# A hybrid attention layer on one core: where GpSimd's sums, the first gate loads and the forget gates' chain stand

## The chip, the cores and the metric

The kernel runs on one core of a Trainium2 chip. The metric is the device time of one execution in microseconds. The engines are named as in the profile: PE is TensorE (PEld its weight loads), DVE is VectorE, ACT is ScalarE, POOL is GpSimd, SP is SyncE, which issues most of the DMAs.

## What is computed

One layer over x of 512 rows by 2048 columns. A combined projection gives the queries, keys, values and z of three attention branches, the logits of the forget gates, and three merge gates of 2048 columns each:

```python
h = jnp.einsum('bsd,dn->bsn', x, w_in) + b_in
p = _split_columns(h)
o_fox = fox_attention(..., p["fox_f"])   # bias: c = cumsum(log_sigmoid(f_logit))
o_swa = swa_attention(...)
o_moba = moba_attention(...)
br_fox = merge(o_fox) * silu(p["fox_z"]) @ w_br_fox      # and so for swa, moba
y = sigmoid(p["gate_fox"]) * br_fox + sigmoid(p["gate_swa"]) * br_swa + sigmoid(p["gate_moba"]) * br_moba
out = y @ w_out
x = layer_norm(ALPHA * x + out)
```

All of it is float32.

## The kernel before

A float32 operand is split into a high part (hi, xh, sh; a copy on ScalarE, rounded to float32r) and a low part (lo, xl, sl; a subtraction on VectorE), and one product is three matmuls: high by high, low by high, high by low. `split` (lines 115 to 117) does that, so nearly every matmul waits for a ScalarE and a VectorE operation on its operands.

The first stages are these. **The first projection** (line 434 on) gives the values of two branches and the forget logits in 32 steps n, 16 for each set of 324 columns: `v_step(n)` runs twelve matmuls, four row blocks by three. `prepare_v(n + 2)` splits the weights two steps ahead and, in the first pass, x tile n + 2; hi and lo have three buffers each. SyncE loads x tiles of 256 KB four steps ahead and weight rows (rawv) six steps ahead. Beside it GpSimd forms sums and differences of pairs of x tiles (`x_sums(g)`, lines 221 to 230, four operations each, eight pairs); `x_sums_split(g)` splits them into sh and sl after the steps in `x_done`, and `s1_split(g)` writes one of them into xh and xl. `v_evac` (line 210) adds the bias rows vb to the result in VectorE, copies four forget logits of each row into the tile fg on GpSimd, and returns the store of the values, which ScalarE's queue issues a step later. The rows vb are loaded by GpSimd's queue.

**The gates** (line 474 on) come in six groups of 56 steps m, seven products of eight steps of six matmuls 128x512. The seven products are those of a Strassen-like scheme over a 2 by 2 block matrix; their operands are the loaded blocks rawa, rawb, rawc and rawd, four of 512 KB each in a group, which VectorE combines in place (`combine`, the table `COMBINE`), and the sums sh. `gate_prepare(n)` splits a block two steps ahead into ghi and glo. After some steps VectorE adds a bank of PSUM and a bias row (gbias) into result tiles, and ScalarE takes the sigmoid and stores them. The tiles of gbias share their two buffers with vb. For the first group SyncE's queue loads a, c and d, GpSimd's queue b; later groups are loaded by SyncE during the group before. rawc takes turns with rawv in four buffers; rawa takes the buffers of the sums' results (xsum), so a load of rawa waits for the split of those.

**The forget gates' chain** `forget_bias` (line 374) computes log sigmoid of the 32 logits in each of 128 rows as a generator in six pieces; a `next` in the last group's steps runs one. Its result goes into the tile pair, and `running_sum` (line 551) forms the cumulative sum by four matmuls on TensorE in the projection behind the gates, whose steps are those of a weight stream (four steps of twelve matmuls for each tile of 128 columns).

The order of all instructions is written by hand: each engine runs its own in the order in which the Python code emits them, and a wait at one of them holds all behind it.

Of the kernel before, what the change touches and what calls it, by code (L numbers as in the profile page):

```python
# [8 lines left out]
F32 = mybir.dt.float32  # L9
F32R = mybir.dt.float32r  # L10
AF = mybir.ActivationFunctionType
ALU = mybir.AluOpType

P = 128
S = 512
# [35 lines left out]
GROUPS = [(b, half) for half in range(2) for b in range(3)]  # L51
# [36 lines left out]
def hybrid_kernel(ctx: ExitStack, tc: tile.TileContext, a: dict, out: bass.AP):  # L88
    nc = tc.nc
# [6 lines left out]
    xl = keep.tile([P, KD, S], F32R, tag="bigl", name="xl")  # L96
    fg = keep.tile([P, 6, 32], F32, name="fg")
# [14 lines left out]
    def att_tile(name):  # L112
        return psum.tile([P, S], F32, tag="att", name=name, bufs=5)
# [11 lines left out]
    def at(i, order, f, *args):  # L125
        tasks.setdefault(i, []).append((order, len(tasks.get(i, ())), f, args))
# [6 lines left out]
    def prepare(i):  # L133

        if i >= len(ids) or i in parts:
            return None
        load(i // 2)
        raw = raws[i // 2][:, (i % 2) * S:(i % 2 + 1) * S]
        if i in held:
            hi, lo = held[i]  # L140
        else:
            hi = stage.tile([P, S], F32R, tag="hi", name="hi")
            lo = stage.tile([P, S], F32R, tag="lo", name="lo")
        parts[i] = (hi, lo)
        nc.scalar.activation(hi, raw, AF.Copy)  # L145

        def lower():
            nc.vector.tensor_sub(lo, raw, hi.bitcast(F32))  # L148
            for d in range(1, raw_bufs):
                load(i // 2 + d)  # L150

        return lower
# [54 lines left out]
    flog = fg[:, 0].rearrange("p (a b) -> p a b", b=NH)  # L207
    vacc = [[acc_tile(f"va{i}") for i in range(3)] + [att_tile("va3")], None]

    def v_evac(ps, st):  # L210
        tag = "qqcp"[st] if ps else "q"
        raw = post.tile([P, S], F32, tag=tag, name="vout", bufs=1 if tag == "c" else 2)[:, :NV]
        nc.vector.tensor_add(raw, vacc[ps][st][:, :NV], vb[ps])
        nc.gpsimd.tensor_copy(flog[:, st, 4 * ps:4 * ps + 4], raw[:, 320:])
        return lambda: nc.scalar.dma_start(a["vs"][ps, :, st], raw)


    s1raw, xsum = [], {}
# [33 lines left out]
    def load_gate(sc, q, blk):  # L252
        if sc >= len(GROUPS):
            return
        if q == "c":
            r = stage.tile([P, 1024], F32, tag="raw", name="rawc", bufs=raw_bufs)
        else:
            r = (rawd if q == "d" else rawp).tile([P, 1024], F32, tag=q, name="raw" + q)
        raw_of[sc, q, blk] = r
        (nc.gpsimd if sc == 0 and q == "b" else nc.sync).dma_start(r, a["wa"][(sc * 4 + "abcd".index(q)) * 4 + blk])  # L260

    def stationary(name, g):
        if name == "a11":
# [22 lines left out]
    def combine(sc, out, x, y, blk, op):  # L286
        o, p, q = (raw_of[sc, k, blk] for k in (out, x, y))
        nc.vector.tensor_tensor(out=o, in0=p, in1=q, op=op)


    COMBINE = {}
# [12 lines left out]
    sums_of, evs = {}, {}  # L304
# [18 lines left out]
    def gate_bias(sc):  # L323
        for n in range(2):
            evs[sc, "bias", n] = post.tile([P, S], F32, tag="bias", name="gbias")
            nc.gpsimd.dma_start(evs[sc, "bias", n], a["bg"][2 * sc + n:2 * sc + n + 1].to_broadcast([P, S]))

    def tile_of(sc, name, tag, u):
        if (sc, name, u) not in evs:
# [65 lines left out]
    forget = forget_bias()  # L395
# [14 lines left out]
    def gate_ahead(n):  # L410
        if n >= items:
            if n - items < 2:
                prepare(n - items)()
            return
        sc, m = divmod(n, 56)
        if m in COMBINE and sc + (m == 54) < len(GROUPS):
            combine(sc + (m == 54), *COMBINE[m])
        gate_prepare(n)
        if sc == len(GROUPS) - 1 and m in (51, 53, 55):
            load((m - 51) // 2)  # L420
        for q, blk in LOADS.get(m, ()):
            load_gate(sc + 1, q, blk)
        for q, blk in LOADS.get(m + 56, ()):
            load_gate(sc, q, blk)
# [5 lines left out]
        begin[(22, 23, 25, 27)[blk]] = ("a", blk)  # L430
        begin[26 + 2 * blk] = ("c", blk)
    stores = []
    x_done = [11, 13, 15, 17, 20, 22, 24, 26]
    for n in range(2 * KD):
        if n + 4 < KD:
            load_x(n + 4)
        if n % 2 == 0 and n // 2 + 3 < KD:
            load_v(n // 2 + 3)
        if n in begin:
            load_gate(0, *begin[n])  # L440
        if n == 29:
            combine(0, *COMBINE[54])
        if n + 2 < 2 * KD:
            prepare_v(n + 2)
        else:
            gate_ahead(n + 2 - 2 * KD)
        if n == 5:
            for j in range(2):
                nc.gpsimd.dma_start(vb[j], a["bv"][j:j + 1].to_broadcast([P, NV]))
        if n == KD:  # L450
            vacc[1] = [att_tile(f"vc{i}") for i in range(4)]
        if n >= 8 and n % 2 == 0 and n < 24:
            x_sums(n // 2 - 4)
            if n >= 16:
                load_gate(0, "b", (n - 16) // 2)
        v_step(n)
        for f in stores:
            f()
        stores = []
        if n in x_done:  # L460
            x_sums_split(x_done.index(n))
        if n >= KD + 2 and n % 2 == 0:
            s1_split((n - KD - 2) // 2)
        if KD + 1 <= n < KD + 5:
            stores.append(v_evac(0, n - KD - 1))
# [5 lines left out]
    for n in range(items):  # L471
        sc, m = divmod(n, 56)
        gate_ahead(n + 2)
        gate_step(n)
        for f in stores:
            f()
        stores = [v_evac(1, n)] if n < 4 else []
        if n == 0:
            s1_split(7)
        if n == 4:  # L480
            gate_bias(0)
        if m == 52 and sc + 1 < len(GROUPS):
            gate_bias(sc + 1)
        for g, d in ((sc - 1, m + 56), (sc, m)):
            for f, args in AFTER.get(d, ()) if g >= 0 else ():
                f(g, *args)
        if sc == len(GROUPS) - 1:
            if m in (44, 47, 49, 51, 53, 54):
                next(forget, None)
            if m == 42:  # L490
                x_back_load()
            if m in (50, 52):
                x_back((m - 50) // 2)
# [57 lines left out]
    def running_sum(pair):  # L551
        csum = att_tile("csum")
        for st in range(4):
            nc.tensor.matmul(csum[:, st * P:], pair[:, st], tri[:, :S - st * P], start=(st == 0), stop=(st == 3))
        rows = work.tile([P, S], F32, tag="tmp", name="rows")
        nc.scalar.activation(rows[:NH], csum[32:32 + NH], AF.Copy)
        nc.vector.tensor_add(rows[:NH], csum[:NH], rows[:NH])
        nc.sync.dma_start(a["scratch"], rows[:NH])
# [246 lines left out]
    for p in range(4):  # L805
        q, k, z = [], [], []
# [10 lines left out]
    for p in range(4):  # L817
        q, z = [], []
# [16 lines left out]
    for p in range(4):  # L835
        q, k, z = [], [], []
# [179 lines left out]
            at(7 + st, 3, v_split, ps, st, dests[ps])  # L1016
    nl = []
    at(3, 6, make_pair)
    at(4, 8, lambda: running_sum(nl[0]))
    at(12, 7, lambda: nc.vector.tensor_scalar(nsink, sinkc, -1.0, None, op0=ALU.mult))  # L1020
    mix0 = last_att + 1
    at(mix0, 0, open_mix)
# [103 lines left out]
```

## Time and profile before

| | us |
|---|---|
| median of three runs | 1350.73 (1349.37 to 1351.04) |
| profiled execution | 1350.06 |
| its span in the profile | 1348.4 |
| TensorE busy | 1326.3 |
| VectorE busy | 903.6 |
| ScalarE busy | 649.8 |
| GpSimd busy | 188.1 |

Matmuls are pipelined and their ends are modelled, so TensorE's starts are read, not its ends: where the starts of two like matmuls lie farther apart than elsewhere, TensorE waited. A row in the timeline has its start, its duration, and in brackets how long the engine stood idle and what ended that. "issue" there means that nothing in the profile shows the cause.

### The profile page before, as it was taken

How to read it: one execution, taken by the hardware profiler on the slowest of the kernel's cores; microseconds unless marked ns; L12 is line 12 of the kernel's file. 1: busy time of each engine (PE TensorE's matmuls, PEld its weight loads, DVE VectorE, ACT ScalarE, POOL GpSimd, SP SyncE). 2: the span in 40 equal slices, each digit the busy share in tenths (PEclk: the TensorE clock that was granted, in tenths of full speed). 3: DMA queues.
4: the chain of work that ended last, by engine and by line, in shares of the span. 5: the costliest groups of instructions: out<-in, count | busy, mean ns of one | idle time of the engine just before them, and what ended most of it. 6: DMA issues, size and time to landing. Idle time of an engine off the chain costs nothing.

```text
span 1348.4 us, 18408 instructions
## 1 busy us (share of the span) xinstructions
PE 1326.3 (98%) x6435; PEld 1116.7 (83%) x6435; DVE 903.6 (67%) x1629; ACT 649.8 (48%) x1189; POOL 188.1 (14%) x254
## 2 busy tenths in 40 slices
PE   8999999999999999999999999999999999999996
PEld 7978788888888887788888998888888888888885
DVE  6878888888888978565656555555556666532456
ACT  4544645555554646556564555565654222222231
POOL 5540000000000000012222323121130000000005
PEclk8999999999999999999999999999999999999998
DMA  7733517071542603433322222222225555463323
GB/s 234 230 143 127 193 40 281 17 271 57 195 133 92 229 24 119 160 106 95 94 86 79 83 83 79 79 79 79 78 79 187 187 187 185 147 225 98 94 94 125
DMA packets 57676, 174.43 MB, mean 129 GB/s; under 512 B 6552, under 2 KB 8088, under 8 KB 56816
## 3 DMA queue, kind: packets, MB, share of 16 engines
q1 hardware_dynamic: 46960, 147.44, 33.3%
q10 hardware_dynamic: 8064, 13.91, 2.7%
q0 software_dynamic: 2560, 11.90, 2.6%
q8 instruction: 50, 0.82, 0.2%
q14 instruction: 42, 0.34, 0.1%
HBM read 155.12 MB, written 18.12 MB: 128 GB/s over the span
## 4 chain that ended last, share of the span: by engine, by line
PE 94%; DMA 2%; DVE 2%; issue 1%; ACT 1%; SPq 0%; DVEq 0%; POOL 0%; ACTq 0%
PE br L879 10%; PE h L751 9%; PE h L753 9%; PE h L752 9%; PE beta L321 4%; PE beta L320 4%; PE beta L319 4%; PE o L941 4%; PE o L940 4%; PE o L939 4%; PE gamma L321 3%; PE alpha L321 3%; PE gamma L319 3%; PE gamma L320 3%; PE alpha L320 3%; PE alpha L319 3%
## 5 line engine op out<-in xcount | busy, mean ns | idle before, releaser
L145 ACT ACTIVATE hi<-raw 128x512 fp32r<-128x512 f32 x248 | 156.3, 631 | 324.3 <-PE o L940 97.5
L148 DVE TENSOR_TENSOR lo<-raw,hi 128x512 fp32r<-128x512 f32 x248 | 174.1, 706 | 151.9 <-ACT hi L145 127.4
L751 PE MATMUL h<-xh,hi 128*128 128x512 f32 x528 | 208.0, 394 | 0.0
L753 PE MATMUL h<-xh,lo 128*128 128x512 f32 x528 | 206.6, 391 | 0.0
L752 PE MATMUL h<-xl,hi 128*128 128x512 f32 x528 | 206.1, 390 | 0.0
L753 PEld LDWEIGHTS h<-xh,lo 128*128 128x128 f32 x528 | 99.1, 188 | 22.0 <-DVE lo L148 0.5
L752 PEld LDWEIGHTS h<-xl,hi 128*128 128x128 f32 x528 | 99.3, 188 | 18.6
L751 PEld LDWEIGHTS h<-xh,hi 128*128 128x128 f32 x528 | 99.2, 188 | 18.4
L667 POOL TENSOR_SCALAR lt<-lt,st 128x128 f32<-128x128 f32 (+2 forms) x96 | 71.1, 740 | 288.8 <-DVE st L666 286.9
L116 ACT ACTIVATE ghi<-rawd 128x512 fp32r<-128x512 f32 x96 | 60.7, 632 | 70.9 <-DVE glo L117 52.1
L116 ACT ACTIVATE ghi<-rawb 128x512 fp32r<-128x512 f32 x96 | 60.7, 632 | 69.9 <-DVE glo L117 48.0
L116 ACT ACTIVATE ghi<-rawa 128x512 fp32r<-128x512 f32 x96 | 60.7, 633 | 59.3 <-PE alpha L320 25.1
L117 DVE TENSOR_TENSOR glo<-rawd,ghi 128x512 fp32r<-128x512 f32 x96 | 66.3, 691 | 27.2 <-ACT ghi L116 24.9
L939 PE MATMUL o<-hi,yh 128*128 128x512 f32 (+1 forms) x212 | 81.8, 386 | 0.0
L940 PE MATMUL o<-hi,yl 128*128 128x512 f32 (+1 forms) x212 | 81.7, 385 | 0.0
L941 PE MATMUL o<-lo,yh 128*128 128x512 f32 (+1 forms) x212 | 81.7, 385 | 0.0
L117 DVE TENSOR_TENSOR glo<-rawb,ghi 128x512 fp32r<-128x512 f32 x96 | 66.3, 690 | 18.9 <-ACT ghi L116 17.7
L321 PE MATMUL alpha<-glo,xh 128*128 128x512 f32 x192 | 75.6, 394 | 2.7 <-DVE glo L117 2.5
L321 PE MATMUL beta<-glo,sh 128*128 128x512 f32 x192 | 74.8, 390 | 1.4 <-DVE glo L117 1.4
L879 PE MATMUL br<-hi,ozh 128*128 128x512 f32 x192 | 75.3, 392 | 0.0
L879 PE MATMUL br<-lo,ozh 128*128 128x512 f32 x192 | 74.8, 390 | 0.0
L319 PE MATMUL alpha<-ghi,xh 128*128 128x512 f32 x192 | 74.8, 390 | 0.0
(230 smaller groups left out, 3121.0 us busy)
## 6 DMA issues: line engine op xcount, KB each, us to landing
raw<-in_ws SPq DMA_DIRECT2D x130, 512.0 KB, 3.5
rawa<-in_wa SPq DMA_DIRECT2D x24, 512.0 KB, 5.1
rawc<-in_wa SPq DMA_DIRECT2D x24, 512.0 KB, 5.7
rawd<-in_wa SPq DMA_DIRECT2D x24, 512.0 KB, 5.6
sig<-gate_tiles SPq DMA_DIRECT2D x48, 256.0 KB, 3.9
rawb<-in_wa SPq DMA_DIRECT2D x20, 512.0 KB, 3.6
rawv<-in_wv SPq DMA_DIRECT2D x15, 324.0 KB, 3.5
xraw<-in_xT SPq DMA_DIRECT2D x16, 256.0 KB, 5.0
```

Of the source, the lines that this page charges most:

```text
L116: nc.scalar.activation(hi, raw, AF.Copy)
L145: nc.scalar.activation(hi, raw, AF.Copy)
L148: nc.vector.tensor_sub(lo, raw, hi.bitcast(F32))
L319: nc.tensor.matmul(o, sth[:, us], hi, start=first, stop=False, skip_group_check=True)
L321: nc.tensor.matmul(o, sth[:, us], lo, start=False, stop=last, skip_group_check=True)
L751: nc.tensor.matmul(accs[t], hi[:, cc], xh[:, k], start=(k == 0), stop=False)
L752: nc.tensor.matmul(accs[t], hi[:, cc], xl[:, k], start=False, stop=False)
L753: nc.tensor.matmul(accs[t], lo[:, cc], xh[:, k], start=False, stop=(k == KD - 1))
L879: nc.tensor.matmul(bracc[g, st], o[:, 4 * b + kt, ss], w, start=(kt == 0 and n == 0), stop=(kt == 3 and n == 2))
L939: nc.tensor.matmul(o, yb["h"][:, k, sl], hi, start=(k == 0), stop=False)
L940: nc.tensor.matmul(o, yb["l"][:, k, sl], hi, start=False, stop=False)
L941: nc.tensor.matmul(o, yb["h"][:, k, sl], lo, start=False, stop=(k == KD - 1))
```

## The change

The change moves the following. GpSimd's loads of the value bias rows vb and its sums now stand behind a copy of one column of xl of x tile 8 (counted from 0) into an unused place of fg, so they wait for that split. The loads of rawa in the first group go from SyncE's queue to GpSimd's. The forget logits are copied on ScalarE, behind the store of the values, and no longer on GpSimd. The bias rows of the first group's gates are loaded by SyncE's queue; those of the later groups stay with GpSimd's. In the first group the combinations of b for blocks 1 to 3 stand one step later, and four of the eight splits of the sums stand one step earlier. The pieces of the forget chain run in step 6 of the first group and step 18 of the others, and the running sum is one step of the weight stream later.

```diff
--- before.py
+++ after.py
@@ -211,8 +211,12 @@
         tag = "qqcp"[st] if ps else "q"
         raw = post.tile([P, S], F32, tag=tag, name="vout", bufs=1 if tag == "c" else 2)[:, :NV]
         nc.vector.tensor_add(raw, vacc[ps][st][:, :NV], vb[ps])
-        nc.gpsimd.tensor_copy(flog[:, st, 4 * ps:4 * ps + 4], raw[:, 320:])
-        return lambda: nc.scalar.dma_start(a["vs"][ps, :, st], raw)
+
+        def store():
+            nc.scalar.dma_start(a["vs"][ps, :, st], raw)
+            nc.scalar.activation(flog[:, st, 4 * ps:4 * ps + 4], raw[:, 320:], AF.Copy)
+
+        return store
 
 
     s1raw, xsum = [], {}
@@ -257,7 +261,7 @@
         else:
             r = (rawd if q == "d" else rawp).tile([P, 1024], F32, tag=q, name="raw" + q)
         raw_of[sc, q, blk] = r
-        (nc.gpsimd if sc == 0 and q == "b" else nc.sync).dma_start(r, a["wa"][(sc * 4 + "abcd".index(q)) * 4 + blk])
+        (nc.gpsimd if sc == 0 and q in "ab" else nc.sync).dma_start(r, a["wa"][(sc * 4 + "abcd".index(q)) * 4 + blk])
 
     def stationary(name, g):
         if name == "a11":
@@ -323,7 +327,7 @@
     def gate_bias(sc):
         for n in range(2):
             evs[sc, "bias", n] = post.tile([P, S], F32, tag="bias", name="gbias")
-            nc.gpsimd.dma_start(evs[sc, "bias", n], a["bg"][2 * sc + n:2 * sc + n + 1].to_broadcast([P, S]))
+            (nc.gpsimd if sc else nc.sync).dma_start(evs[sc, "bias", n], a["bg"][2 * sc + n:2 * sc + n + 1].to_broadcast([P, S]))
 
     def tile_of(sc, name, tag, u):
         if (sc, name, u) not in evs:
@@ -413,8 +417,9 @@
                 prepare(n - items)()
             return
         sc, m = divmod(n, 56)
-        if m in COMBINE and sc + (m == 54) < len(GROUPS):
-            combine(sc + (m == 54), *COMBINE[m])
+        c = m - 1 if n in (1, 3, 5) else -1 if n in (0, 2, 4) else m
+        if c in COMBINE and sc + (c == 54) < len(GROUPS):
+            combine(sc + (c == 54), *COMBINE[c])
         gate_prepare(n)
         if sc == len(GROUPS) - 1 and m in (51, 53, 55):
             load((m - 51) // 2)
@@ -430,7 +435,7 @@
         begin[(22, 23, 25, 27)[blk]] = ("a", blk)
         begin[26 + 2 * blk] = ("c", blk)
     stores = []
-    x_done = [11, 13, 15, 17, 20, 22, 24, 26]
+    x_done = [10, 13, 15, 17, 19, 21, 23, 26]
     for n in range(2 * KD):
         if n + 4 < KD:
             load_x(n + 4)
@@ -444,7 +449,8 @@
             prepare_v(n + 2)
         else:
             gate_ahead(n + 2 - 2 * KD)
-        if n == 5:
+        if n == 6:
+            nc.gpsimd.tensor_copy(fg[:, 5, :1], xl[:, 8, :1].bitcast(F32))
             for j in range(2):
                 nc.gpsimd.dma_start(vb[j], a["bv"][j:j + 1].to_broadcast([P, NV]))
         if n == KD:
@@ -479,14 +485,14 @@
             s1_split(7)
         if n == 4:
             gate_bias(0)
+        if n == 6 or m == 18 and sc:
+            next(forget, None)
         if m == 52 and sc + 1 < len(GROUPS):
             gate_bias(sc + 1)
         for g, d in ((sc - 1, m + 56), (sc, m)):
             for f, args in AFTER.get(d, ()) if g >= 0 else ():
                 f(g, *args)
         if sc == len(GROUPS) - 1:
-            if m in (44, 47, 49, 51, 53, 54):
-                next(forget, None)
             if m == 42:
                 x_back_load()
             if m in (50, 52):
@@ -1016,7 +1022,7 @@
             at(7 + st, 3, v_split, ps, st, dests[ps])
     nl = []
     at(3, 6, make_pair)
-    at(4, 8, lambda: running_sum(nl[0]))
+    at(5, 8, lambda: running_sum(nl[0]))
     at(12, 7, lambda: nc.vector.tensor_scalar(nsink, sinkc, -1.0, None, op0=ALU.mult))
     mix0 = last_att + 1
     at(mix0, 0, open_mix)
```

GpSimd, from its first load on: bT is a small load, L449 the value bias rows, L227 to L230 the first sum of x tiles 0 and 1. Before:

```order
L204 DMA bT<-in_bT 128x64
L449 DMA vb_115<-in_bv 128x324
L449 DMA vb_116<-in_bv 128x324
L227 TENSOR_TENSOR s1raw<-xraw 128x256
L228 TENSOR_TENSOR xsum<-s1raw,xraw 128x256
L229 TENSOR_TENSOR xsum<-xraw 128x256
L230 TENSOR_TENSOR xsum<-xraw,xsum 128x256
```

With the change:

```order
L204 DMA bT<-in_bT 128x64
L453 COPY fg<-xl 128x1
L455 DMA vb_115<-in_bv 128x324
L455 DMA vb_116<-in_bv 128x324
L231 TENSOR_TENSOR s1raw<-xraw 128x256
L232 TENSOR_TENSOR xsum<-s1raw,xraw 128x256
L233 TENSOR_TENSOR xsum<-xraw 128x256
L234 TENSOR_TENSOR xsum<-xraw,xsum 128x256
```

A copy that reads xl stands ahead of the two loads and, through them, of all the sums.

SyncE, the end of the first projection's loads (rawv), then the first group's gate blocks; rawb at the end is the second group's. Before:

```order
L175 DMA rawv<-in_wv 128x648 x6
L260 DMA rawa<-in_wa 128x1024 x2
L175 DMA rawv<-in_wv 128x648
L260 DMA rawa<-in_wa 128x1024
L260 DMA rawc<-in_wa 128x1024
L260 DMA rawa<-in_wa 128x1024
L260 DMA rawc<-in_wa 128x1024 x3
L260 DMA rawd<-in_wa 128x1024 x4
L260 DMA rawb<-in_wa 128x1024 x2
```

With the change:

```order
L175 DMA rawv<-in_wv 128x648 x7
L264 DMA rawc<-in_wa 128x1024 x4
L264 DMA rawd<-in_wa 128x1024 x4
L330 DMA gbias<-in_bg 128x512 x2
L264 DMA rawb<-in_wa 128x1024 x2
```

The four rawa are gone from between rawv and rawc, and the two gbias stand behind rawd.

VectorE, around the first gate steps, with the combinations (rawb<-rawc,rawb), the low parts glo, the value results vout and the last of the sums' splits into xl. Before:

```order
L117 TENSOR_TENSOR glo<-rawa,ghi 128x512
L288 TENSOR_TENSOR rawb<-rawc,rawb 128x1024
L117 TENSOR_TENSOR glo<-rawa,ghi 128x512
L213 TENSOR_TENSOR vout<-vc_491,vb_116 128x324
L117 TENSOR_TENSOR xl<-s1raw,xh 128x256
L117 TENSOR_TENSOR glo<-rawa,ghi 128x512
L213 TENSOR_TENSOR vout<-vc_492,vb_116 128x324
L288 TENSOR_TENSOR rawb<-rawc,rawb 128x1024
L117 TENSOR_TENSOR glo<-rawa,ghi 128x512
L213 TENSOR_TENSOR vout<-vc_493,vb_116 128x324
L117 TENSOR_TENSOR glo<-rawa,ghi 128x512
L213 TENSOR_TENSOR vout<-vc_494,vb_116 128x324
```

With the change:

```order
L117 TENSOR_TENSOR xl<-s1raw,xh 128x256
L292 TENSOR_TENSOR rawb<-rawc,rawb 128x1024
L117 TENSOR_TENSOR glo<-rawa,ghi 128x512 x2
L213 TENSOR_TENSOR vout<-vc_492,vb_116 128x324
L117 TENSOR_TENSOR xl<-s1raw,xh 128x256
L292 TENSOR_TENSOR rawb<-rawc,rawb 128x1024
L117 TENSOR_TENSOR glo<-rawa,ghi 128x512
L213 TENSOR_TENSOR vout<-vc_493,vb_116 128x324
L117 TENSOR_TENSOR glo<-rawa,ghi 128x512
L213 TENSOR_TENSOR vout<-vc_494,vb_116 128x324
L292 TENSOR_TENSOR rawb<-rawc,rawb 128x1024
L117 TENSOR_TENSOR glo<-rawa,ghi 128x512
```

The combination that stood ahead of the third glo and of the vout of its step comes behind them, and so for the two after it.

## Rows read from the trace of the kernel before

**Rows 1.** The page, busy time of TensorE: us, share of the span, instructions.
```profile
PE 1326.3 (98%) x6435; PEld 1116.7 (83%) x6435; DVE 903.6 (67%) x1629; ACT 649.8 (48%) x1189; POOL 188.1 (14%) x254
```

**Rows 2.** Timeline of TensorE: start, duration, line, operands, [idle before <-releaser]; step beginnings.
```profile
4.76 0.61 PE L245 MATMUL va<-hi,xh 128*128 128x324 f32 x1
...
10.74 0.64 PE L245 MATMUL va<-hi,xh 128*128 128x324 f32 x1 [3.30 <-ACT xh L116]
...
29.25 0.31 PE L245 MATMUL va<-hi,xh 128*128 128x324 f32 x1
...
69.73 0.39 PE L319 MATMUL alpha<-ghi,xh 128*128 128x512 f32 x1
...
83.44 0.39 PE L319 MATMUL beta<-ghi,sh 128*128 128x512 f32 x1
...
96.03 0.39 PE L319 MATMUL alpha<-ghi,xh 128*128 128x512 f32 x1
...
106.91 0.39 PE L319 MATMUL beta<-ghi,sh 128*128 128x512 f32 x1
```

**Rows 3.** Timeline of TensorE, the last product of the last group and after it.
```profile
522.79 0.50 PE L319 MATMUL gamma<-ghi,sh 128*128 128x512 f32 x1 [0.15 <-ACT ghi L116]
...
536.07 0.39 PE L751 MATMUL h<-xh,hi 128*128 128x512 f32 x1
...
550.63 0.82 PE L554 MATMUL csum<-tri,pair 128*128 128x512 f32 x4 [0.77 <-issue]
```

**Rows 4.** Windows: busy us of PE, PEld, DVE, ACT, POOL, granted clock, DMA share, GB/s.
```profile
10.00:20.00 10.00, 9.13 (x42) 8.50 (x43) 7.62 (x9) 5.35 (x11) 9.59 (x11) 0.69 0.88 325
```

**Rows 5.** Timeline of GpSimd at the start; DMA queues from 4.5 to 10.5.
```profile
2.25 1.10 POOL L449 DMA_DIRECT2D vb<-in_bv  x2
...
q1 hardware_dynamic: 592, 1.17, 53.1%
q0 software_dynamic: 97, 0.33, 30.3%
```

**Rows 6.** Timeline of VectorE and of GpSimd, x tiles in the first projection.
```profile
10.72 0.73 DVE L117 TENSOR_TENSOR xl<-xraw,xh 128x512 fp32r<-128x512 f32 x1 [4.19 <-ACT xh L116]
...
22.07 1.22 DVE L117 TENSOR_TENSOR xl<-xraw,xh 128x512 fp32r<-128x512 f32 x1
...
24.16 1.23 DVE L117 TENSOR_TENSOR xl<-xraw,xh 128x512 fp32r<-128x512 f32 x1
...
21.75 0.99 POOL L227 TENSOR_TENSOR s1raw<-xraw 128x256 f32<-128x256 f32 x1
...
25.94 0.98 POOL L227 TENSOR_TENSOR s1raw<-xraw 128x256 f32<-128x256 f32 x1
```

**Rows 7.** Waits of the DMA queue of SyncE, 30 to 170: us in total, times, longest.
```profile
SPq L260 <- DVE sl L117: 7.9, 2, 5.6
```

**Rows 8.** Timeline of VectorE and of GpSimd, the start of the gates.
```profile
69.86 1.23 DVE L288 TENSOR_TENSOR rawb<-rawc,rawb 128x1024 f32<-128x1024 f32 x1 [3.48 <-DMA rawc<-in_wa]
...
72.55 1.22 DVE L288 TENSOR_TENSOR rawb<-rawc,rawb 128x1024 f32<-128x1024 f32 x1
73.68 0.68 DVE L117 TENSOR_TENSOR glo<-rawa,ghi 128x512 fp32r<-128x512 f32 x1
74.28 0.48 DVE L213 TENSOR_TENSOR vout<-vc,vb 128x324 f32<-128x324 f32 x1
74.69 0.41 DVE L117 TENSOR_TENSOR xl<-s1raw,xh 128x256 fp32r<-128x256 f32 x1
...
92.29 0.69 DVE L335 TENSOR_TENSOR q<-alpha,gbias 128x512 f32<-128x512 f32 x1 [2.35 <-DMA gbias<-in_bg]
...
79.31 8.74 POOL L214 COPY fg<-vout 128x4 f32<-128x4 f32 x1 [0.42 <-DVE vout L213]
88.00 1.08 POOL L326 DMA_DIRECT2D gbias<-in_bg  x2
```

**Rows 9.** Timeline of ScalarE, last group.
```profile
517.71 1.28 ACT L378 ACT_TABLE_LOAD   x1
```

## The prediction

> **What bounds the kernel now.** I read the busy times of the page first, then TensorE's rows in order of time, then what GpSimd, VectorE and SyncE do where TensorE's rows lie too far apart. TensorE is busy for 98% of the span [rows 1], so a change pays only where its matmuls start later than the matmul before them allows. In the first projection (32 steps n = 0 to 31 of twelve 128x324 matmuls) the reader should see an undisturbed pitch and compare the rest with it. From step 9 at 29.25 to the first gate matmul at 69.73 [rows 2] 23 steps take 40.48, so one is 1.76. All 32 would take 56.3. They take 69.73 - 4.76 = 64.97, 8.7 too much, all of it ahead of step 9. In the gates one product of eight steps takes 106.91 - 96.03 = 10.88 undisturbed; the first two take 13.71 and 12.59 [rows 2]: 2.83 and 1.71 too much. The last product of the last group takes 13.28 [rows 3], 2.40 too much. The matmul of the running sum then waits 0.77 [rows 3]. That is 16.4 us in five places, the ceiling of what this change can win. The end of the kernel is not touched.
>
> **Part 1: the v bias rows leave the start.** Before, GpSimd issues two broadcasts at 2.25 [rows 5]. Between 4.5 and 10.5 its queue moves 0.33 MB and holds 30.3% of the 16 engines' time, against 53.1% for SyncE's 1.17 MB [rows 5]: twice the engine time per byte. Step 1 waits until 10.74 for x tile 1 [rows 2]. The granted clock shows what that idle costs besides: 0.69 on average between 10 and 20 [rows 4], so a good part of it at the lower level, 1.2 GHz. With the change these broadcasts stand behind a copy that reads x tile 8, so they start at about 19. The gain on SyncE's loads is bounded below by the share, 0.303 x 6 = 1.8 us, and above by all of the wait: step 0 could end at 7.3, so 3.4. I take the upper end, since x tile 1 stands first among the loads still queued there and waits for the slowest engine. I leave 0.7 of delay at step 2, whose weight rows are queued behind x tiles 1 to 3.
>
> Also VectorE is alone until then. Before, GpSimd's sums are under way from step 1 on, and each of VectorE's subtractions waits for one operation of GpSimd: from xl to xl, with lo between, it takes 24.16 - 22.07 = 2.09, and xl takes 1.22 where it took 0.73 alone [rows 6]. 2.09 is longer than a step, so steps 4 to 9 follow VectorE. Afterwards steps 1 to 9 are TensorE's: step 9 at 7.4 + 8 x 1.76 + 0.7 = 22.2, 7.0 earlier than 29.25.
>
> **Part 2: the sums come later.** What was taken from steps 2 to 9 is late next in steps 10 to 17. x tile 8 is split in step 6 (about 17); its xl is done at 18.8, and GpSimd's copy and the two issues (1.10, [rows 5]) take until 20.2. A sum of four operations takes 25.94 - 21.75 = 4.19 [rows 6]. Beside them VectorE has tiles 10 to 15, 6 x 2.09, and one subtraction of the sums that now comes a step earlier (768 columns; 1.5 with its wait, an estimate from xl's 512): 14.0 from 20.8, to 34.8. Step 15 wants the last at 22.2 + 6 x 1.76 + 0.1 = 32.9: 2.0 lost. The eight sums end at 20.2 + 8 x 4.19 + 4 x 0.54 for the loads between them (an issue as at 88.00, [rows 8]) = 56, and the split of the last one is due on ScalarE in step 26, at about 55. So the later splits arrive just in time or a little late, and ahead of the hi parts of the next steps on ScalarE; I put 1.3 there. Bounds for the whole: 0 (the pairs hide in the two steps by which they run ahead) and 7. So the first gate step comes at 22.2 + 40.5 + 3.3 = 66.0: **3.7 won** of 8.7.
>
> **Part 3: the start of the gates.** Before, the c loads stand on SyncE behind a loads that wait for VectorE's sl (7.9 us in two waits, [rows 7]). VectorE then waits 3.48 for a c block at 69.86 [rows 8], and TensorE lags for eight steps. Now the a loads are on GpSimd, c waits only for its own buffer, and the subtractions b = c - b for the blocks 1 to 3 stand one step later. From the second of them to the first a = a + b VectorE has four combinations (1.13 each by the pitch in [rows 8]), six glo (0.60), four vout (0.41) and one xl (0.4): 10.1 us, with 0.9 idle for ScalarE, from 2 us ahead of the first gate step. Step 6 wants its glo at 8.6 and gets it at 9.0; the new small operation and Exp in step 6 cost about 0.2 by step 10. So 0.7 is left of 2.83: **2.1 won** (bounds 0 and 2.8).
>
> The second product lost 1.71 because VectorE waited until 92.29 for the bias row; GpSimd issued it at 88.00, held by a copy of 128x4 that took 8.74 [rows 8]. The copies are on ScalarE now, behind its store DMAs, and small beside its ghi; SyncE issues the rows in step 4 as soon as the last vout has freed the buffer, with nothing behind them until step 35. They have 9 us to land where 4.3 sufficed: **1.7 won** (bounds 1.0, if the pile of the first product moves there, and 1.7).
>
> **Part 4: the forget chain.** Its six pieces go from the last group's end to one in each group. There they took an Exp with a table load of 1.28 [rows 9] and another back, and some 20 small operations, beside the split of the loaded-back x. In their new places, step 18 of each later group, VectorE has no combination. One table load remains in the first group, as before. **2.0 won** of 2.40 (bounds 1.3 and 2.4). The running sum comes one projection step of 2.7 later, its pair is ready at 550.6, so its 0.77 goes: **0.8 won** (bounds 0.5 and 0.9). What follows it, the rows' store and reload, is wanted six steps later.
>
> The sum: 3.7 + 2.1 + 1.7 + 2.0 + 0.8 = 10.3. The profiled execution took 1350.06 (span 1348.4), so 1339.8; it lies 0.67 under the median of three, 1350.73, whose spread is 1.7. Against the median: 1340.4.
>
> **Rivals.** First, **GpSimd yields**: at 79.31 VectorE runs unslowed while GpSimd's copy is held [rows 8]. If the sums yield in the same way without being late, the 3.3 of part 2 vanish: 1337.1. Against it stands the alternation of [rows 6], in which both slow down.
>
> Second, **the early tile isn't freed**: the lag of x tile 1 stays because of SyncE's own loads (53% of the engines' time, with two more x tiles and two weight blocks behind it), the clock drops again, and only VectorE's quiet remains. Step 9 then comes at about 26, part 2 takes back 3.3, and the first stage wins nothing: 1350.7 - 6.6 = 1344.1.
>
> Third, **a new wait in the gates** that eats two thirds of parts 3 and 4, such as ScalarE held by the stores that its copies now stand behind: 1346.
>
> Fourth, the other side, **GpSimd's queue starves**: three of the four a loads are issued from about 56 on, between VectorE's last sums and its combinations. An issue takes 0.54 when it runs; held like the copy, it takes 8.7. Two so held are 17.4, less the 4 us between landing and use: 13.4 lost, 1353.8. It decides from 10.3 + 4 = 14.3 us of hold. Against it: the two issues at 88.00 ran in 1.08 [rows 8], and VectorE has gaps in the steps from 18 to 28. The Trainium skill's page "SBUF — State Buffer", section "SBUF: two separate sides", says that GpSimd cannot write the descriptors of its DMAs while VectorE holds the port pair that they share, and advises to issue from ScalarE or SyncE; by that rule the move of the a loads is a risk and the move of the bias rows a cure. The trace shows the copy held, and no load held.
>
> **How the numbers follow.** Forecast 0.62 (1338 to 1342.5 by the middle of the bounds), GpSimd yields 0.13, the early tile isn't freed 0.13, a new wait 0.06, starved 0.06. The likeliest gives 1340.4. The range takes in the first two rivals and leaves out the last two: 1335.5 to 1345. About 0.2%, 2.7 us, is what a measurement of this kernel can tell from no change: faster than 1348.0 holds the forecast, the first two rivals and half of the third, 0.90; within, 0.05; slower, 0.05.
>
> **What would show it.** Right: step 1 of the projection by 8, the granted clock near 1.00 from 10 to 20, step 9 near 22; subtractions of 1.2 in x tiles 10 to 15; the first gate matmul near 66; no wait for gbias; no table load in the last group and its last product at 10.9. Wrong: x tile 1 still landing near 10, ScalarE waiting long for GpSimd's xsum from step 13 on, VectorE or ScalarE waiting for rawa.

## The result and the profile after

The changed kernel takes 1342.6 us (median of 4 executions, 1342.5 to 1343.81) against 1350.15 for the kernel before, run beside it (1349.37 to 1351.04): a ratio of 0.9946, 95% interval 0.9934 to 0.9958. That is faster by 7.5 us; 1340.4 was forecast, 10.3 less than the 1350.73 known then. Its profiled execution took 1342.68, with a span of 1341.0, against 1350.06 and 1348.4. So 7.4 of the span are to be found.

On the page TensorE is busy for 99%, 3 us less than in [rows 1]; where the time went is not to be seen there.

```profile
PE 1323.1 (99%) x6435; PEld 1115.8 (83%) x6435; DVE 906.3 (68%) x1629; ACT 647.6 (48%) x1195; POOL 177.2 (13%) x249
```

TensorE's timeline of the changed kernel shows it; the columns are those of [rows 2, 3]. The rows are the starts of steps 1, 4, 9, 13, 14, 17, 23 and 25 of the projection, then of the first four products of the gates, of the last product of the last group, of what follows it, and of the running sum.

```profile
7.39 0.41 PE L249 MATMUL va<-hi,xh 128*128 128x324 f32 x1
...
14.23 0.31 PE L249 MATMUL va<-hi,xh 128*128 128x324 f32 x1
...
23.19 0.31 PE L249 MATMUL va<-hi,xh 128*128 128x324 f32 x1
...
30.35 0.31 PE L249 MATMUL va<-hi,xh 128*128 128x324 f32 x1
...
33.79 0.31 PE L249 MATMUL va<-hi,xh 128*128 128x324 f32 x1
...
40.19 0.31 PE L249 MATMUL vc<-hi,xh 128*128 128x324 f32 x1
...
51.84 0.31 PE L249 MATMUL vc<-hi,xh 128*128 128x324 f32 x1
...
57.26 0.31 PE L249 MATMUL vc<-hi,xh 128*128 128x324 f32 x1
...
69.61 0.39 PE L323 MATMUL alpha<-ghi,xh 128*128 128x512 f32 x1
...
81.27 0.39 PE L323 MATMUL beta<-ghi,sh 128*128 128x512 f32 x1
...
92.37 0.39 PE L323 MATMUL alpha<-ghi,xh 128*128 128x512 f32 x1
...
103.25 0.39 PE L323 MATMUL beta<-ghi,sh 128*128 128x512 f32 x1
...
518.36 0.39 PE L323 MATMUL gamma<-ghi,sh 128*128 128x512 f32 x1
...
529.65 0.39 PE L757 MATMUL h<-xh,hi 128*128 128x512 f32 x1
...
545.99 0.74 PE L560 MATMUL csum<-tri,pair 128*128 128x512 f32 x4
```

Read against before, row by row: step 9 comes 6.06 earlier (23.19 against 29.25), and yet the first gate product only 0.12 earlier (69.61 against 69.73). What the start of the projection gained, its later steps gave back. One execution tells this stage only to some 0.3: runs 5 to 9 below, whose projection is the changed kernel's but for a few gate loads and combinations at its end, have the first gate product at 69.25 to 69.89. The first product then takes 11.66 against 13.71, the second 11.10 against 12.59, the last one 11.29 against 13.28, and no wait stands ahead of the running sum any more. So the change won 0.1 in the projection, 3.5 at the start of the gates and 2.0 in the last product. Of the rest, 0.3 is the product ahead of the last one (11.20 before, 10.88 after), 0.4 lies between, and 1.1 behind the last product: the projection that begins there (h) is first interrupted for the attention's own matmuls and goes on at 563.31 after and 570.84 before, 33.66 and 34.77 behind that product.

The clock fell no more between 10 and 20, where [rows 4] had 0.69 (columns as there):

```profile
10.00:20.00 10.00, 9.69 (x64) 9.46 (x64) 7.41 (x13) 6.01 (x13) 0.35 (x2) 1.00 1.02 378
```

Where the projection lost its gain is to be seen on VectorE, GpSimd and TensorE between 24 and 56. The first two rows are the starts of two sums on GpSimd, then three subtractions of VectorE in a row, then the two longest waits of TensorE:

```profile
24.85 0.99 POOL L231 TENSOR_TENSOR s1raw<-xraw 128x256 f32<-128x256 f32 x1
...
29.05 1.45 POOL L231 TENSOR_TENSOR s1raw<-xraw 128x256 f32<-128x256 f32 x1
...
28.42 1.49 DVE L117 TENSOR_TENSOR sl<-xsum,sh 128x768 fp32r<-128x768 f32 x1
29.83 1.03 DVE L117 TENSOR_TENSOR lo<-rawv,hi 128x324 fp32r<-128x324 f32 x1
30.78 1.22 DVE L117 TENSOR_TENSOR xl<-xraw,xh 128x512 fp32r<-128x512 f32 x1
...
32.05 0.41 PE L250 MATMUL va<-hi,xl 128*128 128x324 f32 x1 [1.39 <-DVE xl L117]
...
55.66 0.41 PE L251 MATMUL vc<-lo,xh 128*128 128x324 f32 x1 [1.54 <-DVE lo L117]
```

A sum takes 4.20 there (29.05 - 24.85), as in [rows 6], and xl takes 1.22, as it did between the early sums. TensorE waits for VectorE's subtractions. Four steps from step 13 take 9.84 (40.19 - 30.35) where four at the pitch of their neighbours, 1.79, take 7.16: 2.7 lost. From step 22 to step 26 another 2.7 go.

### The profile page after: what moved, and what is told of

Its sections match the earlier page's. It is cut to its first block, busy times and chain, and to the rows that moved or that the text cites. A ratio compares the mean times of both kernels' runs of the same rounds, so it can differ in the third digit from the quotient of the medians.

```text
span 1341.0 us, 18413 instructions
## 1 busy us (share of the span) xinstructions
PE 1323.1 (99%) x6435; PEld 1115.8 (83%) x6435; DVE 906.3 (68%) x1629; ACT 647.6 (48%) x1195; POOL 177.2 (13%) x249
## 4 chain that ended last, share of the span: by engine, by line
PE 97%; DVE 1%; issue 0%; DMA 0%; SPq 0%; ACT 0%; DVEq 0%; ACTq 0%
PE br L885 10%; PE h L757 9%; PE h L759 9%; PE h L758 9%; PE beta L325 5%; PE beta L323 5%; PE beta L324 5%; PE o L947 4%; PE o L945 4%; PE o L946 4%; PE gamma L325 3%; PE alpha L325 3%; PE gamma L323 3%; PE gamma L324 3%; PE alpha L323 3%; PE alpha L324 3%
```

## The experiments

Four questions: what freed x tile 1; what took the gain of the projection back; which edits made the start of the gates shorter; and whether the running sum had to be moved. The first four runs are timed, beside 15 executions of the kernel before (median 1350.62). Run 11 is timed beside 7 more. Runs 5 to 10 and 12 are single executions, in which the stretch in question is read from TensorE's rows. A product of the gates repeats closely: the first takes 11.62 to 11.66 in the changed kernel and in runs 2 to 5, 8 and 10 to 12.

**1. The bias rows moved, nothing else.**

```
 (kernel before)
-        if n == 5:
-            for j in range(2):
-                nc.gpsimd.dma_start(vb[j], ...)
...
             x_sums(n // 2 - 4)
+            if n == 14:
+                for j in range(2):
+                    nc.gpsimd.dma_start(vb[j], ...)
```

> The kernel before with one edit: the two broadcasts of the v bias rows are issued by GpSimd behind its fourth x sum; the sums wait for nothing new. Theory (the broadcasts hold x tile 1 back; the wait of the sums for tile 8 only moves the loss): step 1 of the projection starts at 7.4 instead of 10.74, the granted clock from 10 to 20 is near 1.00, the sums run from about 7 on, step 9 comes near 25, nothing is late in steps 13 to 25, and the first gate matmul comes at 65.5 to 67 instead of 69.73: 1346 to 1347.5. Rival 1 (tile 1 is held by SyncE's own loads): step 1 stays near 10.7 and the time at 1350. Rival 2 (early sums are what must go): step 1 at 7.4, but step 9 stays beyond 27 and the first gate matmul near 69: 1349.5.

Measured: 1345.61 us, ratio 0.9964 (0.9952 to 0.9977). TensorE's timeline, steps 1 and 9 and the first gate matmul:

```profile
7.87 0.41 PE L245 MATMUL va<-hi,xh 128*128 128x324 f32 x1 [1.02 <-ACT xh L116]
...
26.39 0.31 PE L245 MATMUL va<-hi,xh 128*128 128x324 f32 x1
...
67.61 0.39 PE L319 MATMUL alpha<-ghi,xh 128*128 128x512 f32 x1
```

Step 1 is 2.9 earlier than in [rows 2], and the granted clock from 10 to 20 is 1.00, so the broadcasts were what held x tile 1; both rivals fall. The sizes were not quite the theory's: step 9 and the first gate matmul are later than it said (near 25, 65.5 to 67), the time is a little below its range. Steps 4 to 8 run at 2.06 to 2.12, at VectorE's pace beside the sums. Behind step 9 nothing is lost: 67.61 - 26.39 = 41.22, 23 steps of 1.79. The first gate matmul is 2.1 earlier than before, where the whole change with its wait made it 0.1. Two of the six executions took 1347.39 and 1347.54, four 1345.19 to 1345.74. The rows are of the one with 1347.54 and show 2.5 of the 5.0 between the medians; where the rest lies is not shown.

**2. The change without the wait.**

```
 (changed kernel)
-        if n == 6:
-            nc.gpsimd.tensor_copy(fg[:, 5, :1], xl[:, 8, :1]...)
-            for j in range(2):
-                nc.gpsimd.dma_start(vb[j], ...)
...
             x_sums(n // 2 - 4)
+            if n == 14:
+                (the same two loads)
```

> The changed kernel without the wait of GpSimd for x tile 8; the v bias rows are issued behind the fourth sum. Theory (the late start of the sums is what took the won time back): the sums run from 7 to about 43 instead of 21 to 57, no loss in steps 13 to 16 and 22 to 25, first gate matmul at 65.5 to 67 instead of 69.61: 1338.5 to 1340. Rival (it makes no difference when the sums run, since they slow VectorE by the same sum anywhere): first gate matmul at 69 to 70, 1342 to 1343.

Measured: 1340.73 us, ratio 0.9926 (0.9911 to 0.9941). TensorE's timeline, step 9 and the first gate matmul, and the window from 10 to 20:

```profile
25.96 0.31 PE L249 MATMUL va<-hi,xh 128*128 128x324 f32 x1
...
67.65 0.40 PE L323 MATMUL alpha<-ghi,xh 128*128 128x512 f32 x1
...
10.00:20.00 10.00, 8.76 (x46) 8.53 (x47) 10.00 (x11) 5.01 (x11) 9.77 (x11) 0.83 0.87 306
```

Early sums cost 2.8 up to step 9 (25.96 against 23.19), with some clock (0.83), but only 0.5 behind it, where the wait cost 5.3 of the same 23 steps (69.61 - 23.19 = 46.42 against 23 x 1.79 = 41.2). So the wait cost 2.0 in all (69.61 against 67.65). The time and the first gate matmul are a little above the theory's ranges (1338.5 to 1340, 65.5 to 67). Steps 13 to 16 lose nothing, as it said, steps 22 to 25 still 0.5. The sums don't end by 43 as I wrote, but at 51: the fifth waits 7.05 for the buffer that a split of VectorE frees.

**3. The bias rows back at the start, the wait kept.**

```
 (changed kernel)
-        if n == 6:
+        if n == 5:
+            (the two loads of vb)
+        if n == 6:
             nc.gpsimd.tensor_copy(fg[:, 5, :1], xl[:, 8, :1]...)
-            (the two loads of vb)
```

> The changed kernel with the two broadcasts of the v bias rows back at the start of GpSimd's queue; the sums still wait for x tile 8. Theory (the broadcasts hold x tile 1 back): step 1 at 10.7 instead of 7.39, a granted clock near 0.7 from 10 to 20, step 9 at 26.5 or later, first gate matmul at 72 to 73: 1345 to 1346. Rival (GpSimd's early sums, not the broadcasts, made the start late): step 1 at 7.4 and 1342.6 as before this edit.

Measured: 1347.01 us, ratio 0.9976 (0.9967 to 0.9985); some 4 slower than the change. TensorE's timeline, steps 1 and 9 and the first gate matmul, and the window from 10 to 20:

```profile
10.94 0.64 PE L249 MATMUL va<-hi,xh 128*128 128x324 f32 x1 [3.01 <-ACT xh L116]
...
28.34 0.31 PE L249 MATMUL va<-hi,xh 128*128 128x324 f32 x1
...
74.25 0.39 PE L323 MATMUL alpha<-ghi,xh 128*128 128x512 f32 x1
...
10.00:20.00 10.00, 8.97 (x40) 8.62 (x41) 5.09 (x9) 4.90 (x11) 0.00 (x0) 0.66 0.90 326
```

With GpSimd's sums out of the way (POOL 0.00) and the broadcasts there, x tile 1 is late again and the clock is down to 0.66. So the broadcasts alone do it. The size came out above the theory: the first gate matmul at 74.25, not 72 to 73, and the time above its 1345 to 1346.

**4. The sums on VectorE.**

```
 (changed kernel, x_sums: four times)
-        nc.gpsimd.tensor_tensor(out=s1, in0=e[:, hi2], ...)
+        nc.vector.tensor_tensor(out=s1, in0=e[:, hi2], ...)
...
-    x_done = [10, 13, 15, 17, 19, 21, 23, 26]
+    x_sum = [1, 3, 5, 8, 12, 16, 18, 21]
+    x_done = [11, 14, 16, 18, 20, 22, 24, 26]
...
-        if n >= 8 and n % 2 == 0 and n < 24:
-            x_sums(n // 2 - 4)
+        if n in x_sum:
+            x_sums(x_sum.index(n))
```

> The changed kernel with the eight x sums on VectorE itself (steps 1, 3, 5, 8, 12, 16, 18, 21; their splits in steps 11, 14, 16, 18, 20, 22, 24, 26). GpSimd has only DMA issues left in the projection. Theory (what is lost in steps 13 to 25 is VectorE and GpSimd slowing each other): no VectorE operation is slowed, xl stays at 0.73 and lo near 0.5; the sums cost VectorE some 8 x 4 x 0.4 = 12.8, four of them in the stretch in which it waits for loads anyway; first gate matmul at 65 to 66.5, 1338 to 1340. Rival (VectorE has simply too much to do: 12.8 in its own operations is as much as the 14 by which it was slowed): first gate matmul at 69 to 71, 1342 to 1344.

Measured: 1337.68 us, ratio 0.9903 (0.9889 to 0.9918). First the groups of VectorE's subtractions up to 70 in the changed kernel (shapes, count, busy us, mean ns, idle before and its releaser), then the same groups up to 64, one of the four groups of sums, step 9 and the first gate matmul in this one:

```profile
L117 DVE TENSOR_TENSOR lo<-rawv,hi 128x324 fp32r<-128x324 f32 x32 | 22.9, 721 | 7.4 <-ACT hi L116 6.8 <-DMA xraw<-in_xT 0.6
L117 DVE TENSOR_TENSOR xl<-xraw,xh 128x512 fp32r<-128x512 f32 x15 | 14.1, 939 | 1.4 <-ACT xh L116 1.3
L117 DVE TENSOR_TENSOR sl<-xsum,sh 128x768 fp32r<-128x768 f32 x8 | 10.4, 1299 | 1.9 <-ACT sh L116 1.9
```

```profile
L117 DVE TENSOR_TENSOR lo<-rawv,hi 128x324 fp32r<-128x324 f32 x32 | 15.7, 492 | 7.8 <-ACT hi L116 7.7
L117 DVE TENSOR_TENSOR xl<-xraw,xh 128x512 fp32r<-128x512 f32 x15 | 10.3, 688 | 0.3 <-ACT xh L116 0.3
L117 DVE TENSOR_TENSOR sl<-xsum,sh 128x768 fp32r<-128x768 f32 x8 | 7.6, 955 | 1.3 <-ACT sh L116 1.2
L232 DVE TENSOR_TENSOR xsum<-s1raw,xraw 128x256 f32<-128x256 f32 x8 | 3.4, 425 | 0.3
...
22.79 0.31 PE L249 MATMUL va<-hi,xh 128*128 128x324 f32 x1
...
64.02 0.39 PE L323 MATMUL alpha<-ghi,xh 128*128 128x512 f32 x1
```

The subtractions cost 22.9 + 14.1 + 10.4 = 47.4 beside GpSimd's sums and 15.7 + 10.3 + 7.6 = 33.6 without: 13.8 less. The sums themselves cost VectorE 4 x 3.4 = 13.6. So the rival's arithmetic was right, VectorE has as much to do, and its conclusion was wrong: 64.02 - 22.79 = 41.23 is 23 x 1.79, nothing is lost. What differs is when. Between 10 and 20 VectorE is now busy for 9.90, where it had 7.41 in the changed kernel, and from 20 to 60 for 34.3 instead of 36.9 (windows of 10 us, summed). Three of the sums lie between 11 and 20, in time that VectorE spent waiting in the changed kernel. Little of that was for loads, as the waits there from 10 to 20 show (us in total, times, longest):

```profile
ACT hi L116 <- PE va L250: 4.0, 5, 0.8
DVE lo L117 <- ACT hi L116: 1.5, 3, 0.6
DVE lo L117 <- DMA xraw<-in_xT: 0.6, 1, 0.6
```

VectorE waited for ScalarE's hi, and ScalarE for TensorE to be done with a buffer of hi: VectorE was ahead of TensorE. The first gate matmul and the time are even below the theory's ranges (65 to 66.5, 1338 to 1340).

**5. The gate bias rows on GpSimd again.**

```
 (changed kernel)
-            (nc.gpsimd if sc else nc.sync).dma_start(evs[sc, "bias", n], ...)
+            nc.gpsimd.dma_start(evs[sc, "bias", n], ...)
```

> The changed kernel with the first group's gate bias rows issued by GpSimd again; the forget gate copies stay on ScalarE. Theory (the copy held on GpSimd, not its queue, made the rows late before): GpSimd is idle when the last vout frees the buffer, issues the rows in about 1.1 near 77, VectorE doesn't wait for gbias and the second product stays at 11.1. Rival (GpSimd's issues themselves are held while VectorE is busy): the rows are issued late, VectorE waits 1 to 2.4 for gbias, the second product takes 12.0 to 12.8.

Measured: second product 91.99 - 80.87 = 11.12. GpSimd's timeline:

```profile
76.98 0.54 POOL L330 DMA_DIRECT2D gbias<-in_bg  x1 [14.68 <-DVE vout L213]
```

It issues the row as soon as vout frees the buffer. The theory holds: GpSimd's queue wasn't what made the row late.

**6, 7 and 9. The a loads on SyncE, the combinations unshifted, and both.**

```
 (6 and 9)
-        (nc.gpsimd if sc == 0 and q in "ab" else nc.sync).dma_start(r, ...)
+        (nc.gpsimd if sc == 0 and q == "b" else nc.sync).dma_start(r, ...)
 (7 and 9)
-        c = m - 1 if n in (1, 3, 5) else -1 if n in (0, 2, 4) else m
+        c = m
```

> The changed kernel with the first group's a loads on SyncE again. Theory (the a loads, which wait for VectorE's splits of the sums, hold the c loads behind them): SyncE waits for sl again by several us, VectorE waits 2 to 3.5 for rawc at its first combinations, and the first product takes 12.7 to 13.7 in place of 11.66. Rival (the later combinations alone took the lag away): 11.6 to 11.9.

> The changed kernel with the three combinations c - b of the first group's blocks 1 to 3 back in steps 0, 2 and 4 of the gates, not a step later. Theory (part of the first product's gain is from the shift): VectorE is later by one combination of 1.2 in the first steps and the first product takes 12.0 to 12.8. Rival (the c loads were the whole lag): 11.6 to 11.8.

> The changed kernel with both undone at once: the first group's a loads on SyncE, and the combinations c - b of blocks 1 to 3 in steps 0, 2 and 4. Each alone cost 0.25 to 0.3 of the 2.0 won in the first product. Theory of the prediction (these two make the lag, and either one hides the other): 12.9 to 13.7 for the first product. Rival (the forget gate copies on GpSimd made most of it): the two add up, 12.0 to 12.4.

Measured for the first product: 81.71 - 69.80 = 11.91 with the a loads on SyncE, 81.28 - 69.33 = 11.95 with the combinations unshifted, against 11.66; for both, TensorE's timeline:

```profile
69.54 0.39 PE L323 MATMUL alpha<-ghi,xh 128*128 128x512 f32 x1
...
82.39 0.39 PE L323 MATMUL beta<-ghi,sh 128*128 128x512 f32 x1
```

That is 12.85, just below the theory's 12.9 to 13.7. Each edit alone is nearly unneeded (0.25 and 0.29; run 6 lies just above its rival's range, run 7 between its theory's and its rival's), both together are worth 1.19. In run 6 the mechanism of the prediction is there, in the waits of SyncE's queue from 40 to 80 and on VectorE's timeline, but the shifted combinations leave VectorE time for it:

```profile
SPq L264 <- DVE sl L117: 8.8, 2, 6.1
...
66.51 1.22 DVE L292 TENSOR_TENSOR rawb<-rawc,rawb 128x1024 f32<-128x1024 f32 x1 [2.78 <-DMA rawc<-in_wa]
```

Of the 2.05 that the first product gained, 1.2 are these two. The other 0.9 are not accounted for by any single edit that I undid; some 0.25 of it may be the spread of the old gates, whose first product takes 13.46 in run 1.

**8. The running sum back in step 4.**

```
 (changed kernel)
-    at(5, 8, lambda: running_sum(nl[0]))
+    at(4, 8, lambda: running_sum(nl[0]))
```

> The changed kernel with the running sum back in projection step 4. Theory of the prediction (the step was needed): TensorE waits 0.8 for the pair, csum comes 14.4 after the last product and the step after it is late. Rival (the early forget chain alone makes the pair ready: in the changed kernel it is done at 542.7, 13.05 after the last product, and the place in step 4 is at 13.6): no wait, csum 13.6 to 13.7 after the last product, and the shift of the running sum was worth nothing.

Measured on TensorE's timeline, the end of the last product and the running sum:

```profile
529.15 0.39 PE L757 MATMUL h<-xh,hi 128*128 128x512 f32 x1
...
542.77 0.57 PE L560 MATMUL csum<-tri,pair 128*128 128x512 f32 x2
```

It comes 13.62 behind the last product, without a wait. The rival holds: the early forget chain alone takes the wait of [rows 3] away. The projection goes on 33.76 behind the last product, 33.66 in the changed kernel; so the shift is worth at most 0.1.

**10 and 12. The forget gate copies on GpSimd, without and with the bias rows.**

```
+        nc.gpsimd.tensor_copy(flog[:, st, 4 * ps:4 * ps + 4], raw[:, 320:])
+
         def store():
             nc.scalar.dma_start(a["vs"][ps, :, st], raw)
-            nc.scalar.activation(flog[:, st, 4 * ps:4 * ps + 4], raw[:, 320:], AF.Copy)
 (12 besides: the edit of run 5)
```

> The changed kernel with the eight forget gate copies back on GpSimd; the gate bias rows stay on SyncE. For the first product, theory of the prediction (loads and combinations made the lag): 11.6 to 11.9; rival (the copies made it, by slowing VectorE or by holding vout's buffers): 12.5 to 13.7. For the steps 22 to 25 of the projection, where 2.7 are lost: theory (VectorE and GpSimd slow each other): still 2.5 to 3; rival (ScalarE, held by its copies until vout is there, splits too late): below 1, and the first gate matmul near 67.5. For the second product, theory (the copy held the bias rows alone): 11.1, with the rows landed in time; rival (the held copy keeps vout's buffer from p as well): 11.5 to 12.5.

> The changed kernel with the forget gate copies and the first group's gate bias rows both on GpSimd, as before the change. Theory (a copy is held for long only while VectorE, late from the first product, runs its operations back to back; without that lag both may stay on GpSimd): no copy above 2, second product 11.1 to 11.2. Rival (GpSimd as such makes the rows late): a copy held by 5 or more, VectorE waits for gbias, second product 12 to 12.8.

Measured: first product 11.64 in both, second product 11.15 and 11.12. GpSimd's timeline in run 12, the last and longest copy and the rows behind it:

```profile
76.04 1.12 POOL L215 COPY fg<-vout 128x4 f32<-128x4 f32 x1 [1.02 <-DVE vout L213]
77.10 1.07 POOL L331 DMA_DIRECT2D gbias<-in_bg  x2
```

The same copy took 8.74 in [rows 8]. There VectorE, late from the first product, ran combinations and glo without a gap; once that lag is gone, the copy isn't held, and everything may stay on GpSimd. In run 9 the lag is back while copies and rows are moved, and the second product takes 93.53 - 82.39 = 11.14. So with copies and rows moved a lag of that size doesn't reach the second product, and without a lag the move is not needed. With the lag and the copies on GpSimd there are only the kernel before and run 1 (12.59 and 12.65), whose lag is larger. In the projection, steps 22 to 27 (the waits now reach step 26) lose 1.9 in run 10 against 2.7, neither what the theory (2.5 to 3) nor what its rival (below 1) expected: ScalarE, which waits for vout with its copies, has a share of some 0.7; the rest, 1.9, stays without them.

**11. Sums on VectorE, and another order of the first loads.**

```
 (kernel of run 4)
-    for k in range(1, 4):
-        load_x(k)
+    load_x(1)
     load_v(1)
+    load_x(2)
+    load_x(3)
     load_v(2)
```

> The kernel with the sums on VectorE, and one edit more: at the start the weight rows of steps 2 and 3 are loaded ahead of x tiles 2 and 3, not behind them. With the sums on VectorE, step 2 started at 9.61, 2.89 after step 1, since its weight rows were in at 8.1 only, while x tile 3, needed a step later, was in at 7.5. Theory (the order alone): rows in near 7, step 2 at 8.6 to 9.0, step 4 at 12.2 to 12.8 instead of 13.86, first gate matmul at 62.4 to 63 instead of 64.02: 1336 to 1336.8. Rival (x tile 2 then comes as late as the rows did, since the bytes are the same): step 4 at 13.5 or later, 1337.4 to 1338.

Measured: 1337.03 us, ratio 0.99 (0.9884 to 0.9917), not to be told from run 4. TensorE's timeline, steps 1 and 2:

```profile
8.31 0.42 PE L250 MATMUL va<-hi,xh 128*128 128x324 f32 x1 [0.27 <-ACT xh L116]
...
10.79 0.31 PE L250 MATMUL va<-hi,xh 128*128 128x324 f32 x1
```

The theory missed, and the time lies between its range and its rival's (1336 to 1336.8, 1337.4 to 1338). Step 2 follows step 1 by 2.48 instead of 2.89, but step 1 itself is later, 8.31 against 6.72, and step 4 comes at 14.37, not at 12.2 to 12.8 but beyond 13.5, as the rival said. Neither row says why x tile 1 is later with another load behind it; part may be spread, since step 1 starts anywhere from 6.72 to 8.01 in the changed kernel and in runs 1, 2, 4 to 10 and 12, which load the same at the start. Both this version and run 4 beat the changed kernel, by some 5 us.

## Why the prediction was right, and where it wasn't

The time lies in the range and the sign is right, but not by the terms as they were put down. The projection won 0.1 of its 3.7; parts 3 and 4 and what lies around them gave 7.3 for 6.6, of which 0.7 (the product ahead of the last one, and what lies between) was not forecast at all. That the total is only 2.2 off owes something to luck.

**Part 1** holds. Step 1 at 7.39 (7.4 said; that it agrees to 0.01 is luck, as runs 5 to 10 and 12 have it at 7.23 to 8.01), the clock at 1.00, xl alone on VectorE till 20; runs 1 and 3 show from both sides that the broadcasts were the cause. Step 9 came at 23.19, not 22.2: steps 1 to 3 took 6.84 where I gave 3 x 1.76 + 0.7 = 6.0, since steps 1 and 2 each lose some 0.6 between their first and second matmul (7.39 to 8.12 and 9.96 to 10.69, where 0.15 is usual): TensorE waits there for xl of their tile, which the sum left out.

**Part 2** is the term that was mis-sized. I put 3.3 on the later sums, with bounds of 0 and 7; from step 9 to the first gate matmul 46.42 passed, 5.9 more than the 40.48 of before. Of that, 2.7 lie in steps 13 to 16 (2.0 said), 2.7 in steps 22 to 25 (1.3 said) and some 0.5 in a pitch of 1.79 instead of 1.76, which I had not thought of. The mechanism was as written: tiles 10 to 15 at 1.22 a subtraction. I had xl of tile 15 at 34.8 and it was done at 36.2, and I left out that the stores' copies, new on ScalarE, wait there for vout. So of the 3.7 to be won in the projection 0.1 was left. Run 2 shows the sign: early sums cost 2.8 ahead of step 9 and save 4.7 behind it. The wait kept GpSimd out of a stretch in which VectorE had time to spare (busy for 7.41 of the 10 us from 10 to 20, against 10.00 in run 2 and 9.90 in run 4) and put the meeting of the two engines where it had none.

**Part 3** is right in size, 3.5 against 3.8, and in its reading of [rows 7, 8], but not in what it gives to each edit. The 1.7 of the second product was put on moving the copies and the bias rows off GpSimd; by runs 5, 10 and 12 neither move matters once the first product no longer lags. And of the two edits on the first product either one nearly suffices.

**Part 4**: the last product gained 1.99 (2.0 said), and 0.3 more in the product before it. The two table loads near 518 and 520 are gone from the last group. No run puts the chain alone back; but it is the only edit in the last group's steps, run 1, with the chain late, has 13.29 there, and runs 2 to 12, which undo most of the other edits one by one, all have 11.28 to 11.31. The 0.8 put on the running sum's place came (1.1), but from the forget chain: run 8 gives the move at most 0.1.

**The rivals.** GpSimd doesn't yield: xl took 1.22 beside the sums wherever they stood. The early tile was freed. No new wait came in the gates but ScalarE's for the first forget piece, which stands in a first product of 11.66. GpSimd's issues were never held: the four a loads took 0.53 or 0.54 each, one row took 0.54 at 76.98 in run 5, and two rows took 1.07 in run 12, where VectorE ran a combination and two glo beside them. The Trainium skill's page "SBUF — State Buffer", section "SBUF: two separate sides", says that GpSimd cannot write its descriptors while VectorE runs an operation in a two-port mode; the prediction left that condition out, and no run here shows such a hold. What was held for long was a copy, and only where the gates are as before: 8.74 in the kernel before, and 8.74 again in run 1. The price of the third rival was summed wrongly: two thirds of the 6.6 of parts 3 and 4 are 4.4, so 1344.8, inside the range, and not 1346.

Something that looks like a gain isn't one. The second product of the second group takes 12.32 in the kernel before and 11.12 after (147.15 to 158.27). But the runs with the same code there had 11.37 to 12.42, as VectorE waits there more in one execution than in another, for a store or a load. Of the 7.4 such places make up 0.4 net, and no edit is shown to be their cause.

## What to carry to other kernels

Where two engines slow each other down, a wait that keeps them apart pays only if the work it delays has free time later; here it was better to put that work where the slowed engine has time to spare, even on that engine itself. Look first at what shares the DMA engines with the first tile that is needed: two small broadcasts cost 3 us of start and a good part of the clock. And when a later stall hangs on an earlier lag, as the held copy did, undo each edit alone and both together before you give either of them the gain (0.25 and 0.29 alone, 1.19 together).

## What I had not expected of the hardware

The projection has two pitches. Undisturbed steps take 1.79 in the changed kernel from step 4 to step 12 (14.23 to 23.19 is 5 x 1.79) and 1.76 from step 27 on, all at a granted clock of 1.00; before the change they took 1.76 from step 10 on. In run 3 it is 1.76 from step 3, in run 4 1.79 in nearly every step from 4 to 31, and runs 10 and 12, whose code is the same there, have 1.79 and 1.76 between steps 4 and 12. Every change of pitch that I saw came within two steps of a wait of TensorE. It is worth up to 0.9 us over the projection; its cause is open.

GpSimd's sums cost VectorE about as much as doing them itself: its subtractions took 13.8 us longer beside them, and the sums on VectorE took 13.6.
